# Expert rows dealt among queries, choices and gates of a bidirectional encoder block, with 16 pairs of rows held in DRAM

## The chip, the core and the metric

One core of a Trainium2 chip runs the whole layer. The metric is the device time of one execution in microseconds (us), the median of three runs. The engines are named as the profile names them: PE is the matrix engine (PEld its weight loads), DVE is VectorE, ACT is ScalarE, POOL is GpSimd and SP is the engine that issues most transfers. Each engine works through its own list of instructions in order and waits where an operand or a buffer is not ready.

## The reference

512 tokens of width 1024 in float32 pass through a mixer and then through a retrieval layer over 16384 single-neuron experts (128 rows of 128 experts).

```python
h = x
h = h + hybrid_mixer(rmsnorm(h, norm_mix_g), ...)     # HGRN2 + Hyena branches
h = h + peer_ffn(rmsnorm(h, norm_ffn_g), w_q, subkeys, u_tab, v_tab)
return rmsnorm(h, norm_final_g)

def peer_ffn(xn, ...):                                # per token, 8 heads
    s = einsum(queries, subkeys)                      # two lists of 128 scores
    s1, i1 = top_k(s[:, :, 0], 16); s2, i2 = top_k(s[:, :, 1], 16)
    top_s, pos = top_k(all sums s1 + s2, 16)          # 16 experts per head
    g = softmax(top_s)
    act = gelu(xn . u[experts]) * g
    return act . v[experts]
```

## The kernel before, in words

The mixer fills the first 760 us or so; its inner part is not touched. The retrieval layer splits the tokens into four blocks of 128. One block (GTB) is done by gathering the chosen experts' rows of `u` and `v` from DRAM, one expert of every token at a time (256 gathers by POOL, each with one DVE instruction of 1024 columns). The other three (DTB, 384 tokens) are done densely: all 128 expert rows are multiplied, and the gates, which are zero for experts not chosen, pick out the right ones.

A dense **expert row** has two halves. The first (`act_row`) takes 128 experts of `u`: a transfer `uraw` on SP's queue, a split into a high part `uh` (ACT) and a low part `ul` (DVE in the early part, POOL once the last loop runs, `looping`), 24 matmuls of 384 columns into `ps_a` (or `ps_mm` while the queries run), and a gelu on ACT into a tile `gact`. The second half (`combine`) multiplies the gated activations `gh`, `gl` with the split second factors `vh`, `vl` of the same 128 experts: 18 matmuls of 512 columns into `acc`. Activations are kept in a ring of 14 tiles of two rows each; the first KEPT pairs of rows instead go to DRAM (`C.kept`) and are read back as `gkept`.

The stages of the retrieval layer, in order:

1. **Queries** (`queries`): 16 projections of 24 matmuls, for each one the scores (L1099), and three times the sixteen best of 128 (`top16`, five DVE instructions). `STEPS` steps of the **choices** (`select`: sums of pairs, the sixteen best, softmax, the experts' numbers) run beside the later queries.
2. **Choices and gates**: for each of the three dense blocks `gates_out` builds the gates' table in 32 batches (DVE: `one`, `own`; ACT: `rows`, `Gs`; PE: 8 matmul records per batch into `ps_g`) and writes it to DRAM as `Gd`. The choices of the next block are mixed in, one step per MIX batches (`mixed`). `weave` adds up the costs that its main work yields and runs one `act_row` each time the sum passes `per`.
3. **The last loop** (`rows`): for each of 128 rows an `act_row` as long as some are left, `split_v`, for each pair `gated` (the gates `gt` read from `Gd`), and `combine`. The choices and gathers of block GTB (`gathered`) are woven in.
4. The final norm and the stores.

Program order is what a scheduling layer makes of this; where a row counts below, it is the built program's order that is shown.

Of the kernel before, what the change touches and what calls it, by code (L numbers as in the profile page):

```python
# [158 lines left out]
def block_kernel(tc, a):  # L159

    nc = tc.nc
    with ExitStack() as ctx:
# [5 lines left out]
        nc.scalar.dma_start(vec, a["vec"])  # L168
# [138 lines left out]
def hyena(C, ctx, xh, xl, raws, fill):  # L307
# [112 lines left out]
    for half in range(D // HC):  # L420
# [33 lines left out]
        for row in (0, FH):  # L454
            nc.scalar.dma_start(fw3[row : row + FH], a["f_w3"].rearrange("f (d c) -> f d c", d=2)[:, :, half * HC : half * HC + HC])
# [346 lines left out]
PER = 2.4  # L802
# [7 lines left out]
def peer(C, ctx, mh, ml):  # L810
# [74 lines left out]
    with tc.tile_pool(name="slw", bufs=2) as sw, tc.tile_pool(name="gb", bufs=1) as gb, \  # L885
            tc.tile_pool(name="go", bufs=3) as go, tc.tile_pool(name="ps_g", bufs=5, space=PSUM) as ps_g:
        def main():
            rest = [[chosen(sw, tb, part) for part in range(2) if part or k >= EARLY] for k, tb in enumerate(DTB)]
            yield from chain(*rest[0])
            for k, tb in enumerate(DTB):  # L890
                nxt = chain(*rest[k + 1]) if k + 1 < len(DTB) else iter(())
# [477 lines left out]
```

## Time and profile before

| what | value |
| --- | --- |
| time, median of 3 runs | 2113.73 us (2110.78 to 2115.68) |
| profiled execution, its own time | 2113.9 us |
| its span, first to last instruction | 2112.1 us |
| PE busy | 2058.7 us |
| DVE busy | 1736.1 us |
| ACT busy | 978.6 us |
| POOL busy | 638.2 us |
| mean granted PE clock, share of full speed | 0.992 |

A matmul counts as busy from its start to its modelled end, and successive ones overlap, so a high busy share does not by itself say that PE delivers all it can. The distance between two starts is the better measure. The clock column is the share of full speed that was granted to PE.

### The profile page before, as it was taken

The page shows a single profiled execution, that of the slowest core. Times are in us where ns is not written, and L with a number is a line of the kernel's source. Part 1 is how long each engine was busy: PE and PEld are TensorE (multiplying, and loading weights), DVE is VectorE, ACT ScalarE, POOL GpSimd, SP SyncE. Part 2 cuts the span into 40 slices and gives each one's busy share as a digit, 9 for nine tenths or more (in the row PEclk, how much of TensorE's full clock was granted, in tenths as well). Part 3 has the DMA queues.
Part 4 walks back from the last instruction along what each step waited for, and adds up shares of the span by engine and source line. Part 5 has one row for each costly group of instructions (what it writes and reads, how often), then busy time and mean ns, then how long its engine had stood idle before and what let it go on. Part 6 is the DMA issues. An engine that isn't in the chain of part 4 may idle for free. (4 is left out here: it accounts for less than half of the span.)

```text
span 2112.1 us, 29790 instructions
## 1 busy us (share of the span) xinstructions
PE 2058.7 (97%) x11109; PEld 1822.7 (86%) x11109; DVE 1736.1 (82%) x3073; ACT 978.6 (46%) x1396; POOL 638.2 (30%) x361
## 2 busy tenths in 40 slices
PE   7999999999999999979999999999999999999998
PEld 6888888888888898879988989989989998998997
DVE  6888764998998546999999988878878879778785
ACT  6555434667665623337766423333333333333333
POOL 0000000000000000000000378877777676666760
PEclk9999999999999999999999999999999999999999
DMA  6212222222212444124547689988888988888884
GB/s 199 80 51 66 70 70 94 67 65 66 70 54 81 120 151 139 61 70 168 202 180 250 192 311 344 327 318 304 321 318 301 317 311 299 316 317 324 296 286 148
DMA packets 153949, 407.68 MB, mean 193 GB/s; under 512 B 12457, under 2 KB 65451, under 8 KB 152140
## 3 DMA queue, kind: packets, MB, share of 16 engines
q1 hardware_dynamic: 110028, 255.98, 35.8%
q0 software_dynamic: 36864, 134.23, 17.6%
q10 hardware_dynamic: 6912, 15.56, 2.1%
q8 instruction: 87, 1.43, 0.3%
q14 instruction: 58, 0.48, 0.1%
HBM read 373.22 MB, written 32.51 MB: 192 GB/s over the span
## 5 line engine op out<-in xcount | busy, mean ns | idle before, releaser
L86 POOL TENSOR_TENSOR ul<-uraw,uh 128x1024 fp32r<-128x1024 f32 x100 | 265.3, 2654 | 589.7 <-DMA uraw<-in_uT 387.6
L95 PE MATMUL ps_a<-pxl,uh 128*128 128x384 f32 x1008 | 343.1, 340 | 0.0
L94 PE MATMUL ps_a<-pxh,uh 128*128 128x384 f32 x1008 | 341.8, 339 | 1.3 <-ACT gact L867 1.2
L980 PE MATMUL acc<-vl,gh 128*128 128x512 f32 x768 | 301.5, 393 | 2.1 <-DVE vl L86 2.1
L979 PE MATMUL acc<-vh,gh 128*128 128x512 f32 x768 | 299.7, 390 | 2.6 <-ACT vh L85 2.6
L981 PE MATMUL acc<-vh,gl 128*128 128x512 f32 x768 | 301.5, 393 | 0.0
L94 PE MATMUL ps_mm<-xh,whi 128*128 128x512 f32 (+1 forms) x656 | 259.1, 396 | 1.5 <-ACT xh L195 1.2
L940 DVE SCALAR_TENSOR_TENSOR xg<-grow,gw,xg 128x1024 f32<-128x1024 f32 x127 | 208.6, 1643 | 63.1 <-DMA grow<-in_v,gidx 62.0
L931 DVE SCALAR_TENSOR_TENSOR grow<-grow,xg 128x1024 f32<-128x1024 f32 x128 | 195.9, 1541 | 73.6 <-DMA grow<-in_u,gidx 73.3
L95 PE MATMUL ps_mm<-xl,whi 128*128 128x512 f32 (+1 forms) x656 | 255.0, 390 | 0.3 <-DVE xl L196 0.3
L85 ACT CAST vh<-vraw 128x1024 fp32r<-128x1024 f32 x128 | 134.3, 1050 | 252.7 <-PE acc L981 179.7
L826 POOL IOTA iota<- 128x512 bf16 x1 | 1.2, 1237 | 754.4 <-DVE gt L281 754.4
L906 POOL DMA_INDIRECT grow<-in_u,gidx x128 | 201.0, 1570 | 41.4 <-issue 19.4
L97 PE MATMUL ps_a<-pxh,ul 128*128 128x384 f32 x1008 | 200.1, 338 | 6.3 <-DVE ul L86 4.1
L85 ACT CAST uh<-uraw 128x1024 fp32r<-128x1024 f32 x128 | 134.7, 1053 | 143.5 <-PE ps_a L95 76.5
L94 PEld LDWEIGHTS ps_a<-pxh,uh 128*128 128x128 f32 x1008 | 191.1, 190 | 6.4 <-ACT gact L867 2.2
L95 PEld LDWEIGHTS ps_a<-pxl,uh 128*128 128x128 f32 x1008 | 190.9, 189 | 3.8
L86 DVE TENSOR_TENSOR vl<-vraw,vh 128x1024 fp32r<-128x1024 f32 x128 | 186.4, 1457 | 8.3 <-ACT vh L85 8.3
L97 PEld LDWEIGHTS ps_a<-pxh,ul 128*128 128x128 f32 x1008 | 176.8, 189 | 8.2 <-DVE ul L86 5.5
L906 POOL DMA_INDIRECT grow<-in_v,gidx x128 | 170.5, 1332 | 32.7 <-issue 18.3
L85 ACT CAST whi<-wraw 128x1024 fp32r<-128x1024 f32 x112 | 117.3, 1050 | 131.0 <-PE ps_mm L95 123.5
L980 PEld LDWEIGHTS acc<-vl,gh 128*128 128x128 f32 x768 | 144.6, 188 | 31.1 <-DVE vl L86 2.9
(414 smaller groups left out, 4188.8 us busy)
## 6 DMA issues: line engine op xcount, KB each, us to landing
uraw<-in_uT SPq DMA_DIRECT2D x128, 512.0 KB, 7.0
vraw<-in_v SPq DMA_DIRECT2D x128, 512.0 KB, 6.3
wraw<-in_w_in SPq DMA_DIRECT2D x80, 512.0 KB, 3.6
Gd<-Gs SPq DMA_DIRECT2D x12, 2048.0 KB, 7.2
gt<-Gd SPq DMA_DIRECT2D x32, 768.0 KB, 8.7
wraw<-in_w_q SPq DMA_DIRECT2D x16, 512.0 KB, 4.0
wraw<-in_w_b SPq DMA_DIRECT2D x8, 512.0 KB, 3.6
wraw<-in_w_a SPq DMA_DIRECT2D x8, 512.0 KB, 4.3
```

What stands on the lines that cost most here:

```text
L85: nc.scalar.copy(hi, src)
L86: return (eng or nc.vector).tensor_sub(lo, src, hi).ins
L94: nc.tensor.matmul(out, ah, bh, start=(i == 0), stop=False)
L95: nc.tensor.matmul(out, *((al, bh) if late else (ah, bl)), start=False, stop=False)
L97: nc.tensor.matmul(out, *((ah, bl) if late else (al, bh)), start=False, stop=(stop and i == n - 1))
L826: nc.gpsimd.iota(iota, pattern=[[1, P], [0, 4]], base=0, channel_multiplier=0, allow_small_or_imprecise_dtypes=True)
L906: nc.gpsimd.indirect_dma_start(out=t, out_offset=None, in_=tab, in_offset=bass.IndirectOffsetOnAxis(ap=gidx[:, j : j + 1], axis=0))
L931: nc.vector.scalar_tensor_tensor(t, t, 1.0, xg, op0=ALU.mult, op1=ALU.mult, accum_out=gdot[:, j : j + 1])
L940: nc.vector.scalar_tensor_tensor(gacc, t, gw[:, j : j + 1], gacc, op0=ALU.mult, op1=ALU.add)
L979: nc.tensor.matmul(acc[k][:, c], gh[:, ts_], vh[:, ds_], start=(r == 0), stop=False)
L980: nc.tensor.matmul(acc[k][:, c], gh[:, ts_], vl[:, ds_], start=False, stop=False)
L981: nc.tensor.matmul(acc[k][:, c], gl[:, ts_], vh[:, ds_], start=False, stop=(r == NK - 1))
```

## The change

The change has four parts.

- **Dealing.** `mixed` now passes on the costs of the choices' steps, which it swallowed before. The choices' costs are scaled by 0.39 (CHOICE) and a batch of gates costs 0.15 (BATCH); `weave` deals one expert row per 1.0. In the queries, one expert row is dealt beside each query from the eighth on, and the first halves of the choices of all three dense blocks run there, two steps per query.
- **Kept pairs.** KEPT goes from 8 to 16, so 16 pairs of rows go to DRAM and back, and LEFT from 3 to 4: 42 expert rows (2 x 16 + 14 - 4) are dealt ahead of the last loop where 27 were.
- **Placing.** The pool of the gates (`gb`) is opened ahead of the choices' pool, and `gt`, `gkept`, `gh`, `gl` move to a pool `pg` of their own that lies where `gb` lay; `pv` (`vl`, `vh`, `vraw`) lies behind it. The order of the first steps in `rows` changes.
- **The start.** The norm's weights come as one row of 1024 values and are spread over the partitions by two matmuls into PSUM, instead of a 512 KB transfer. The scaling of `x` runs in halves of 512 columns. Four small transfers for the filters are issued later.

```diff
@@ mixed
         yield c
         if i % n == n - 1:
-            next(fill, None)
+            yield next(fill, 0.0)
@@ block_kernel, mixer
-        nc.scalar.dma_start(vec, a["vec"])
...
-        gm = n1.tile([P, D], F32, name="gm")
+        gm = n1.tile([1, D], F32, name="gm")
+        gps = [C.ps_x.tile([P, 512], F32, name="ps_x") for _ in range(2)]
...
-                nc.sync.dma_start(gm, a["g_mix"].to_broadcast([P, D]))
+                nc.scalar.dma_start(gm, a["g_mix"])
+                for c, pg in enumerate(gps):
+                    nc.tensor.matmul(pg, C.ones[0:1], gm[:, c * 512 : c * 512 + 512], start=True, stop=True)
...
-            nc.vector.scalar_tensor_tensor(xn, xn, rs, gm, op0=ALU.mult, op1=ALU.mult)
+            for c, pg in enumerate(gps):
+                xc = xn[:, c * 512 : c * 512 + 512]
+                nc.vector.scalar_tensor_tensor(xc, xc, rs, pg, op0=ALU.mult, op1=ALU.mult)
@@ constants
-KEPT = 8
-LEFT = 3
+KEPT = 16
+LEFT = 4
-EARLY = 2
-STEPS = 1
+STEPS = 2
-PER = 2.4
+CHOICE = 0.39
+BATCH = 0.15
@@ peer
-    with tc.tile_pool(name="slw", bufs=2) as sw, tc.tile_pool(name="gb", bufs=1) as gb, \
+    with tc.tile_pool(name="gb", bufs=1) as gb, tc.tile_pool(name="slw", bufs=2) as sw, \
...
-            rest = [[chosen(sw, tb, part) for part in range(2) if part or k >= EARLY] for k, tb in enumerate(DTB)]
-            yield from chain(*rest[0])
+            rest = [(CHOICE * c for c in chosen(sw, tb, 1)) for tb in DTB]
+            yield from rest[0]
...
-        weave(main(), fill, PER)
+        weave(main(), fill, 1.0)
...
-    pv = rowctx.enter_context(tc.tile_pool(name="pv", bufs=2))
+    pg = rowctx.enter_context(tc.tile_pool(name="pg", bufs=2))
+    pv = rowctx.enter_context(tc.tile_pool(name="pv", bufs=AHEAD + 1))
@@ rows
+        for r in range(AHEAD - 1):
+            split_v(r)
+        for _ in range(LEFT - 1):
+            act_row()
+        gated(0)
         act_row()
-        gated(0)
-        for r in range(AHEAD):
-            split_v(r)
-            if r:
-                act_row()
+        split_v(AHEAD - 1)
         gated(1)
@@ queries
-        early = chain(*(chosen(sw, tb, 0) for tb in DTB[:EARLY]))
+        early = chain(*(chosen(sw, tb, 0) for tb in DTB))
...
-            if hp > 7:
+            if hp >= HEADS - 1:
                 run(islice(early, STEPS))
+                next(fill)
@@ gates_out
-        yield 0.4
+        yield BATCH
```

What this does to the lists is seen best where one engine's rows are few. On SP's queue, from the first query weights (`wraw<-in_w_q`) to the first stored gates (`Gd<-Gs`), the program before issues:

```order
L121 DMA wraw<-in_w_q 128x1024 x5
L846 DMA uraw<-in_uT 128x1024 x4
L121 DMA wraw<-in_w_q 128x1024
L846 DMA uraw<-in_uT 128x1024
L121 DMA wraw<-in_w_q 128x1024 x10
L846 DMA uraw<-in_uT 128x1024 x6
L1245 DMA Gd<-Gs 128x4096
```

and the changed program:

```order
L121 DMA wraw<-in_w_q 128x1024 x5
L853 DMA uraw<-in_uT 128x1024 x4
L121 DMA wraw<-in_w_q 128x1024
L853 DMA uraw<-in_uT 128x1024
L121 DMA wraw<-in_w_q 128x1024 x7
L853 DMA uraw<-in_uT 128x1024 x2
L121 DMA wraw<-in_w_q 128x1024
L853 DMA uraw<-in_uT 128x1024
L121 DMA wraw<-in_w_q 128x1024 x2
L853 DMA uraw<-in_uT 128x1024 x15
L1256 DMA Gd<-Gs 128x4096
```

Each `uraw` is one expert row's first factors. 23 of them now stand ahead of the first stored gates, where 11 stood.

On DVE, in the gates, the program before goes from one step of a choice to the next with gates between and an expert row's low part (`ul`) at the end; the rows that follow here are the first of the run, in which a softmax (`mx`, `ex`, `sm`) is mixed with gates (`one`, `own`):

```order
L1167 TENSOR_REDUCE mx<-ctop 128x4
L1175 CAST cpf<-cpos 128x64
L1228 TENSOR_TENSOR one<-iota,tr 128x1024
L1168 TENSOR_TENSOR ex<-ctop,mx 128x64
L1231 TENSOR_TENSOR own<-one,tg 128x512
L1228 TENSOR_TENSOR one<-iota,tr 128x1024 x2
L1231 TENSOR_TENSOR own<-one,tg 128x512
L1170 TENSOR_REDUCE sm<-ex 128x4
L1231 TENSOR_TENSOR own<-one,tg 128x512
L1171 RECIPROCAL sm<-sm 128x4
L86 TENSOR_TENSOR ul<-uraw,uh 128x1024
```

In the changed program the end of the last choice and the gates beside it stand so:

```order
L86 TENSOR_TENSOR ul<-uraw,uh 128x1024
L1183 TENSOR_TENSOR gate<-ex,sm 128x64
L1201 TENSOR_TENSOR exp<-one,ci 128x800
L1192 TENSOR_REDUCE eid<-exp 128x2x8 x3
L1218 CAST ii<-eid 128x128
L1219 TENSOR_SCALAR ii<-ii 128x128
L1239 TENSOR_TENSOR one<-iota,tr 128x1024 x2
L1242 TENSOR_TENSOR own<-one,tg 128x512 x2
L1239 TENSOR_TENSOR one<-iota,tr 128x1024 x2
L1242 TENSOR_TENSOR own<-one,tg 128x512
L86 TENSOR_TENSOR ul<-uraw,uh 128x1024
```

An expert row's low part now closes every handful of choice steps and batches.

On SP's queue at the end of the gates, the program before issues the first second factors (`vraw`) behind the last stored gates, two rows' `uraw` and the first `gt`:

```order
L1245 DMA Gd<-Gs 128x4096
L846 DMA uraw<-in_uT 128x1024 x2
L958 DMA gt<-Gd 128x12x128
L947 DMA vraw<-in_v 128x1024 x3
L846 DMA uraw<-in_uT 128x1024
```

and the changed program:

```order
L1256 DMA Gd<-Gs 128x4096
L853 DMA uraw<-in_uT 128x1024
L958 DMA vraw<-in_v 128x1024 x2
L853 DMA uraw<-in_uT 128x1024
L967 DMA gt<-Gd 128x12x128
```

Two `vraw` now go ahead of `gt`. On PE, five expert rows stand between the last product of the gates and the first `acc` matmul before, and nine in the changed program.

## Rows read from the trace of the kernel before

**Rows 1.** The page, part 1: busy time, share of the span, instructions.

```profile
PE 2058.7 (97%) x11109; PEld 1822.7 (86%) x11109; DVE 1736.1 (82%) x3073; ACT 978.6 (46%) x1396; POOL 638.2 (30%) x361
```

**Rows 2.** Busy time by stretch, us from the span's start.

```profile
core 0: us, PE busy (x) PEld busy (x) DVE busy (x) ACT busy (x) POOL busy (x), PEclk, DMA share, GB/s
818.40:924.70 106.30, 102.60 (x515) 86.08 (x513) 100.74 (x558) 36.67 (x67) 0.00 (x0) 0.98 0.19 60
924.70:1135.10 210.40, 195.63 (x1329) 186.29 (x1330) 208.79 (x541) 152.48 (x255) 0.00 (x0) 0.97 0.50 183
...
1247.00:1330.00 83.00, 83.00 (x415) 74.86 (x416) 74.83 (x84) 28.41 (x36) 70.10 (x38) 1.00 0.96 349
1330.00:2062.00 732.00, 732.00 (x3657) 660.73 (x3656) 599.48 (x507) 260.16 (x305) 518.32 (x297) 1.00 0.87 311
```

**Rows 3.** Timeline of PE: start, length, engine, line, operation, count.

```profile
1132.44 1.95 PE L1238 MATMUL ps_g<-rows,own 128*128 128x128 f32 x16
...
1135.10 0.33 PE L94 MATMUL ps_a<-pxh,uh 128*128 128x384 f32 x1
...
1139.26 0.33 PE L94 MATMUL ps_a<-pxh,uh 128*128 128x384 f32 x1
...
2080.18 0.39 PE L980 MATMUL acc<-vl,gh 128*128 128x512 f32 x1
...
2085.62 0.39 PE L980 MATMUL acc<-vl,gh 128*128 128x512 f32 x1
```

**Rows 4.** PE's groups of one shape, 818.4 to 1135.1 us.

```profile
L1238 PE MATMUL ps_g<-rows,own 128*128 128x128 f32 x768 | 99.7, 283 | 5.9 <-DVE own L1231 3.5 <-ACT rows L1230 1.7 <-ACT Gs L1243 0.4
...
L1099 PE MATMUL ps_x<-sk,qT 128*128 128x128 f32 x128 | 18.9, 295 | 3.1 <-ACT qT L1096 3.0
```

**Rows 5.** DVE's groups in the same stretch.

```profile
L86 DVE TENSOR_TENSOR ul<-uraw,uh 128x1024 fp32r<-128x1024 f32 x25 | 30.3, 1211 | 0.2 <-ACT uh L85 0.2
...
L1253 DVE MAX8 v<-s 128x8 f32<-128x128 f32 x63 | 16.3, 283 | 5.4 <-ACT s L1102 5.4
```

**Rows 6.** One stretch after a wait of PE; columns as in rows 2.

```profile
1067.30:1074.00 6.70, 6.34 (x27) 6.17 (x28) 6.70 (x16) 4.20 (x7) 0.00 (x0) 0.50 0.25 62
```

**Rows 7.** Timeline from the gates' end to the first gathers; in brackets the idle time before.

```profile
1156.00 0.26 ACT L1169 ACTIVATE ex<-ex 128x64 f32<-128x64 f32 x1 [6.43 <-DVE ex L1168]
...
1158.70 0.50 PE L979 MATMUL acc<-vh,gh 128*128 128x512 f32 x1 [2.63 <-ACT vh L85]
...
1221.59 1.54 POOL L906 DMA_INDIRECT grow<-in_u,gidx  x1 [9.68 <-PE ps_a L97]
...
1230.53 2.53 PE L97 MATMUL ps_a<-pxh,ul 128*128 128x384 f32 x8 [2.18 <-POOL ul L86]
```

**Rows 8.** DVE's longest waits, 1235 to 2062 us: total, times, longest.

```profile
DVE grow L931 <- DMA grow<-in_u,gidx: 65.6, 46, 5.6
DVE xg L940 <- DMA grow<-in_v,gidx: 62.0, 46, 5.7
...
DVE gkept L966 <- DMA gkept<-kept: 5.0, 2, 2.5
```

**Rows 9.** Gathered rows: ns min/median/max, first and last start; then the page's means.

```profile
L931 DVE SCALAR_TENSOR_TENSOR grow<-grow,xg x128: 1208/1215/3514, 1229.9 to 1636.8; 128x1024 f32<-128x1024 f32 x128
L940 DVE SCALAR_TENSOR_TENSOR xg<-grow,gw,xg x127: 1270/1285/3453, 1645.8 to 2061.6; 128x1024 f32<-128x1024 f32 x127
...
L86 POOL TENSOR_TENSOR ul<-uraw,uh 128x1024 fp32r<-128x1024 f32 x100 | 265.3, 2654 | 589.7 <-DMA uraw<-in_uT 387.6
...
L940 DVE SCALAR_TENSOR_TENSOR xg<-grow,gw,xg 128x1024 f32<-128x1024 f32 x127 | 208.6, 1643 | 63.1 <-DMA grow<-in_v,gidx 62.0
L931 DVE SCALAR_TENSOR_TENSOR grow<-grow,xg 128x1024 f32<-128x1024 f32 x128 | 195.9, 1541 | 73.6 <-DMA grow<-in_u,gidx 73.3
```

**Rows 10.** Timeline of the start: the first scaling and the first projection.

```profile
7.02 1.28 DVE L228 SCALAR_TENSOR_TENSOR xn<-xn,nrs,gm 128x1024 f32<-128x1024 f32 x1 [6.00 <-ACT nrs L116]
...
14.93 0.58 PE L94 MATMUL ps_mm<-xh,whi 128*128 128x256 f32 x1 [1.16 <-ACT xh L195]
```

More of the change, by code (lines that the diff above doesn't have):

```diff
@@ L172, in block_kernel @@
         C = Ctx()
+        C.fetch_vec = lambda: nc.scalar.dma_start(vec, a["vec"])
         C.nc, C.tc, C.a, C.ident, C.ones, C.vec, C.eps = nc, tc, a, ident, ones, vec, epsc
@@ L215, in mixer @@
         log_table(C)
-        gm = n1.tile([P, D], F32, name="gm")
+        C.fetch_vec()
+        gm = n1.tile([1, D], F32, name="gm")
+        gps = [C.ps_x.tile([P, 512], F32, name="ps_x") for _ in range(2)]
         xns, raws = [], []
@@ L453, in hyena @@
         fw3 = w2.tile([2 * FH, 2, HC], F32, name="fw3", bufs=1)
-        for row in (0, FH):
-            nc.scalar.dma_start(fw3[row : row + FH], a["f_w3"].rearrange("f (d c) -> f d c", d=2)[:, :, half * HC : half * HC + HC])
+        with tc.issue_after(C.turned):
+            for row in (0, FH):
+                nc.scalar.dma_start(fw3[row : row + FH], a["f_w3"].rearrange("f (d c) -> f d c", d=2)[:, :, half * HC : half * HC + HC])
         fw3h = w2.tile([2 * FH, 2, HC], F32R, name="fw3h", bufs=1)
@@ L461, in hyena @@
         decb = w2.tile([P, 2, HC], F32, name="decb", bufs=1)
-        for dr in range(2):
-            o = dr * D + half * HC
-            nc.scalar.dma_start(decb[:, dr], a["f_decay"][:, o : o + HC].to_broadcast([P, HC]))
         with tc.issue_after(C.turned):
+            for dr in range(2):
+                o = dr * D + half * HC
+                nc.scalar.dma_start(decb[:, dr], a["f_decay"][:, o : o + HC].to_broadcast([P, HC]))
             nc.scalar.activation(decb, decb, AF.Abs)
@@ L884, in peer @@
     C.ps_row, C.ps_row_name = ctx.enter_context(tc.tile_pool(name="ps_a", bufs=2, space=PSUM)), "ps_a"
[L885 removed]
+    with tc.tile_pool(name="gb", bufs=1) as gb, tc.tile_pool(name="slw", bufs=2) as sw, \
             tc.tile_pool(name="go", bufs=3) as go, tc.tile_pool(name="ps_g", bufs=5, space=PSUM) as ps_g:
         def main():
[L888 to L889 removed]
+            rest = [(CHOICE * c for c in chosen(sw, tb, 1)) for tb in DTB]
+            yield from rest[0]
             for k, tb in enumerate(DTB):
[L891 removed]
+                nxt = rest[k + 1] if k + 1 < len(DTB) else iter(())
                 yield from mixed(gates_out(C, gb, go, ps_g, k, tb, gate, eid, iota), nxt, MIX)
[L894 to L896 removed]
+        weave(main(), fill, 1.0)
+    pg = rowctx.enter_context(tc.tile_pool(name="pg", bufs=2))
+    pv = rowctx.enter_context(tc.tile_pool(name="pv", bufs=AHEAD + 1))
     swctx = ExitStack()
@@ L945, in split_v @@
     def split_v(r):
+        vl = pv.tile([P, D], F32R, name="vl")
+        vh = pv.tile([P, D], F32R, name="vh")
         raw = pv.tile([P, D], F32, name="vraw", bufs=3)
         nc.sync.dma_start(raw, a["v"][r * P : r * P + P])
-        vh = pv.tile([P, D], F32R, name="vh", bufs=AHEAD + 1)
-        vl = pv.tile([P, D], F32R, name="vl", bufs=AHEAD + 1)
         split(nc, vh, vl, raw)
@@ L956, in gated @@
         if r % GR == 0:
-            gt = pv.tile([P, NG, GR * GQ], F32, name="gt")
+            gt = pg.tile([P, NG, GR * GQ], F32, name="gt")
             nc.sync.dma_start(gt, C.Gd[:, :, r * GQ : (r + GR) * GQ].rearrange("g p x -> p g x"))
@@ L960, in gated @@
         if p in kept:
-            g = pv.tile([P, 2, ND], F32, name="gkept", bufs=1)
+            g = pg.tile([P, 2, ND], F32, name="gkept", bufs=1)
             nc.sync.dma_start(g, C.kept[kept.index(p)])
@@ L966, in gated @@
         nc.vector.tensor_mul(g4, g4, prep["gt"][:, r % GR : r % GR + 2])
-        gh = pv.tile([P, 2, ND], F32R, name="gh", bufs=3)
-        gl = pv.tile([P, 2, ND], F32R, name="gl", bufs=3)
+        gh = pg.tile([P, 2, ND], F32R, name="gh", bufs=3)
+        gl = pg.tile([P, 2, ND], F32R, name="gl", bufs=3)
         split(nc, gh, gl, g)
```

## The prediction

> **What bounds the kernel now.** I read the page's busy shares first, then the stretches, then the spacing of PE's matmuls, then the waits. PE is busy for 97% of the span [rows 1], but that is no proof of a full engine, so I priced its work by the distance between two starts. An expert row's first half takes 1139.26 - 1135.10 = 4.16 us for its 24 matmuls; 24 matmuls of 512 columns take 5.44 us, 0.227 each; 16 gate products end 1.95 us after they begin, about 0.112 apart once the last one's own length (0.283) is taken off [rows 3, 4]. PE's work can't be made less by this change: the same 128 rows, queries and gates are multiplied. Only time in which PE is held up can be won.
>
> From the queries' first scores at 818.4 us to the end of the gates at 1135.1 us the program before takes 316.7 us. PE's work in it: 768 gate records x 0.112 = 86, 128 score records x 0.112 = 14, 14 projections of 24 x 0.227 = 76, 24.8 expert rows x 4.16 = 103 (counted in the built order), transposes 1: together 281 us. So PE loses about 36 us there. DVE is busy for 100.7 + 208.8 = 309.5 us [rows 2], and of what is left 5.4 us is the wait for the first scores [rows 5]. This stage is DVE's. Choices run beside the gates without a row dealt for them, so DVE has work there that PE has nothing to set against.
>
> Two more losses follow. PE waits 2.63 us for the first second factors at 1158.7, because ACT stood 6.43 us before a softmax of the gathered block's choice (`ex`), waiting for DVE, with the cast of `vh` queued behind it; and 2.18 us at 1230.5 for a low part on POOL, which had put five gathers ahead of it from 1221.6 on [rows 7]. Counted as PE's work against the clock, the delay grows from 36 us at 1135 to 48 us at 1247: 12 us, the slower clock after each wait included. Behind a long wait PE runs at half clock, 1.2 GHz in place of 2.4, for some microseconds: a granted share of 0.50 over 6.7 us after the waits around 1065 [rows 6]. From 1247 to 2062 PE is busy without a gap at full clock [rows 2]; the last loop has nothing to win.
>
> **The change, part by part.**
>
> *Dealing.* In the changed order 38 expert rows stand ahead of the last gate product, against 25. PE's work to that point becomes 281 + 13.2 x 4.16 = 336 us. DVE splits each of the 13 (1.21 us, [rows 5]): 309.5 + 13 x 1.21 = 325 us. So over the whole stage PE becomes the bound, by 11 us. That is an average; what decides is where DVE is furthest behind. I added up both engines' work instruction by instruction in each built order, with the spacings of the trace. In the order before, DVE's sum is ahead of PE's by at most 30.7 us, near the gates' end; with the 5.4 us at the start this makes 36, which is what the trace shows, so I trust the same sum for the changed order. There it is 9 us at the first gate products, 11.8 us at worst early in the second block, and negative from the third block on. PE's loss is then 11.8 + 5.4 = 17 us. The same work (38 rows, all gates) cost 316.7 + 13.2 x 4.16 = 371.6 before and costs 336 + 17 = 353 after: **18 us won**. Bounds: 36 won if the small lags vanish in PE's queue; 5 if the choices moved into the queries hold up the scores, or two falls of the clock in which PE is the bound (3.4 us each at most, half of [rows 6]) come on top.
>
> *Placing, and more rows ahead of the last loop.* Nine expert rows instead of five, 37 us of PE's work instead of 21, lie between the last gate product and the first `acc`. The gathered block's choice comes 20 us or more ahead of PE's need in the same sum, and ACT's list has the casts of the first two `vh` ahead of `ex`. The five gathers on POOL still stand in a row, but DVE, which sets the time of their indices, is some 30 us ahead of PE there instead of 15 us behind. Against this, the two first `vraw` are issued only when the last gate products have left their memory, and ACT's cast waits for them in line: a loss of 0 to 5 us, with the clock's share. I take 2 of the 12 us as left: **10 us won**, bounds 4 and 12.
>
> *Kept pairs.* Eight more pairs of 384 KB go to DRAM and back. Of the writes ACT only issues the transfers, hidden in an engine with 152 of 210 us busy [rows 2]. Reading back cost DVE 5.0 us of waits before [rows 8], beside work of PE; twice that stays hidden as long as the last loop is PE's, and if that cover is gone costs 5 us more.
>
> *The last loop.* It has 17 expert rows less (81 against 98 behind the first `acc`), but still all 256 gathers, one every 3.25 us from 1229.9 to 2061.6 [rows 9]. Between those two points PE's work shrinks by about 62 us (15 rows), from 832 to 770. DVE was busy 74.8 + 599.5 = 674 of 815 us from 1247 to 2062 [rows 2] and waited 128 us for gathered rows [rows 8]. The mean of its instructions on gathered rows is 1541 and 1643 ns where the median is 1215 and 1285, with single ones at 3.5 us [rows 9]: they are held up by something. 15 of the 100 low parts leave POOL; if these are what holds DVE, (326 x 128 + 358 x 127) ns / 100 = 0.87 us per low part, 13 us go. DVE then needs 661 in 753 us, 88%, with 92 us left for waits that took 128. It ran at 74.8 of 83 us, 90%, from 1247 to 1330, at 349 GB/s, and PE did not wait once [rows 2]. I take **0**; the bound is the case in which the gathers keep their pace, 62 us lost less the 20 us or so by which DVE may run behind at the end.
>
> The Trainium skill (SBUF — State Buffer, section "SBUF: two separate sides") says that DVE instructions with two SBUF inputs and POOL's share one pair of ports under an exclusive lock, and that the loser blocks for the whole instruction. The 3.5 us in [rows 9] agree with it: 1.2 us of work plus most of a low part's 2.65 us on POOL. By that rule each low part taken from POOL frees at most 2.65 us of DVE, 40 us for 15, and the last loop would have more room than I gave it; the sum would stay as it is.
>
> *The start.* The 512 KB of norm weights leave SP's queue, which brings the first weights of the mixer forward by one transfer; but DVE's list now begins with their low part, ahead of the first scaling, which started at 7.02 us [rows 10]. Eight scalings of 512 columns out of PSUM replace four of 1.28 us; at half the length each they cost the same. The first projection (14.93 us, [rows 10]) needs the same casts on ACT as before. I take 0, bounds 3 us won and 3 lost.
>
> The sum, against the profiled execution's own 2113.9 us (median 2113.7, so nothing to correct): 2113.9 - 18 - 10 + 0 + 0 = **2086 us**. With the bounds of the stages but PE still bound in the loop: 2113.9 - 36 - 12 - 3 = 2063 to 2113.9 - 5 - 4 + 3 + 5 = 2113.
>
> **The rivals.**
>
> *The loop becomes DVE's (slower).* For it: DVE's 83% and 128 us of waits fill 802 of 815 us, and the waits may depend on the gathers' latency, which grows with the DMA engines' load (0.87 to 0.96 in [rows 2]). If the 832 us of gathering don't shrink at all, 62 - 20 = 42 us are lost: 2128. It decides once more than 28 us of the 62 stay. Against it: the 90% from 1247 to 1330. A part of it, 5 to 20 us lost, is more likely than the whole: about 2098.
>
> *The dealing is too coarse.* Choices of the first halves in the queries put three blocks' softmaxes and gelus on ACT in turn, and DVE's lag in the second block could grow by a clock fall each time. Then 5 to 8 us are won there and 4 behind it: 2103.
>
> *Everything fits.* DVE's lags vanish between the rows, and the start gains: 36 + 12 + 1: 2065.
>
> *The change does nothing* because another engine held the stage: ACT is busy 152 of 210 us and its sums stay 70 us or more ahead of PE; I give it nothing.
>
> **The numbers.** Forecast as worked out, 2076 to 2096: 0.55. Everything fits, 2063 to 2076: 0.10. Too coarse, 2096 to 2109: 0.12. Loop partly DVE's, 2090 to 2109: 0.14. Loop fully DVE's, above 2114: 0.07; within 0.2% of before, between these: 0.02. About 0.2% (4 us) is what a measurement of this kernel tells from no change. Faster by more: 0.55 + 0.10 + 0.12 + 0.14 = 0.91, less 0.04 for what no row here shows: 0.87. Same 0.05, slower 0.08. The range runs from 2068 to 2106; half of "everything fits" and about 0.12 above it are left out.
>
> **What would show it.** Right: DVE busy shares near full until the second block of gates and falling in the third, PE without gaps from there; the first `acc` without a wait and without a stretch at half clock near it; gathers every 3.0 us in the loop, DVE's waits for them near 90 us, PE without gaps. Wrong: PE waits for `vl`, `gl` or POOL's `ul` in the loop; `own` waits in the third block; ACT waiting for `vraw` for more than 5 us at the gates' end.

## Result and profile after

The changed kernel takes 2098.5 us (median of 4 runs, 2097.2 to 2101.3) against 2113.6 us (4 runs, 2110.8 to 2115.7) on the same chip: ratio 0.9931, 95% interval 0.9914 to 0.9948. 15 us are won where 28 were forecast. The profiled execution took 2099.15 us, its span 2097.0.

The page of the changed kernel, part 1, and its stretches, with columns as in [rows 1, 2]:

```profile
PE 2051.3 (98%) x11113; PEld 1822.1 (87%) x11113; DVE 1718.4 (82%) x3092; ACT 984.2 (47%) x1400; POOL 597.5 (28%) x346
```

```profile
818.00:924.00 106.00, 105.27 (x552) 91.19 (x551) 100.45 (x514) 46.60 (x72) 0.00 (x0) 1.00 0.32 100
924.00:1000.00 76.00, 67.37 (x355) 63.87 (x354) 71.12 (x314) 29.90 (x45) 0.00 (x0) 0.91 0.27 85
1000.00:1090.00 90.00, 87.81 (x623) 87.45 (x622) 89.64 (x186) 68.04 (x118) 0.00 (x0) 1.00 0.63 220
1090.00:1180.00 90.00, 90.00 (x671) 89.56 (x670) 69.79 (x121) 70.67 (x123) 0.00 (x0) 1.00 0.60 226
1180.00:1240.00 60.00, 53.31 (x279) 51.18 (x277) 58.97 (x199) 25.69 (x32) 20.47 (x7) 0.94 0.70 228
1247.00:1330.00 83.00, 83.00 (x411) 74.21 (x410) 70.17 (x76) 27.89 (x33) 58.08 (x33) 1.00 0.89 316
1330.00:2062.00 732.00, 732.00 (x3612) 654.83 (x3611) 612.28 (x556) 260.94 (x305) 515.14 (x301) 1.00 0.91 328
...
929.52:936.35 6.83, 4.43 (x17) 4.43 (x17) 6.83 (x19) 2.32 (x5) 0.00 (x0) 0.50 0.27 78
1216.24:1223.07 6.83, 6.01 (x19) 6.01 (x20) 6.71 (x21) 2.54 (x5) 2.75 (x1) 0.50 0.52 166
```

The third block of gates (1090 to 1180 us) and the last loop are PE's without a gap. Three places lose time: 924 to 1000, 1180 to 1240, and a spot at 807 just ahead of the first stretch. At each of them PE runs at half clock for a stretch, granted share 0.50 for 6.83 us; there are four such stretches, and the last two lines show two of them. Timelines of the changed kernel (start, length, engine, line, operation; in brackets the idle time before and what ended it) show the waits:

```profile
800.38 0.34 ACTq L1102 DMA_DIRECT2D sk<-in_skT  x1
800.84 1.06 ACTq L1085 DMA_DIRECT2D hd<-h  x1
809.25 1.28 DVE L1088 SCALAR_TENSOR_TENSOR h<-h,prs,gfn 128x1024 f32<-128x1024 f32 x1 [4.29 <-DMA hd<-h]
...
921.15 1.28 ACT L1180 ACT_TABLE_LOAD   x1 [0.39 <-ACT gact L874]
930.19 0.26 ACT L1180 ACTIVATE ex<-ex 128x64 f32<-128x64 f32 x1 [7.76 <-DVE ex L1179]
930.35 1.03 ACT L85 CAST whi<-wraw 128x1024 fp32r<-128x1024 f32 x1
931.29 0.58 ACT L1106 COPY qT<-ps_mm 128x512 f32<-128x512 f32 x1
931.92 2.07 PE L1109 MATMUL ps_x<-sk,qT 128*128 128x128 f32 x8 [5.51 <-ACT qT L1106]
...
934.52 0.60 DVE L1199 TENSOR_TENSOR one<-pio,cpf 128x800 bf16<-128x800 bf16 x1
...
968.26 1.28 ACT L1180 ACT_TABLE_LOAD   x1
969.55 0.26 ACT L1180 ACTIVATE ex<-ex 128x64 f32<-128x64 f32 x1
969.83 1.28 ACT L874 ACT_TABLE_LOAD   x1
971.12 0.49 ACT L874 ACTIVATE gact<-ps_mm 128x384 f32<-128x384 f32 x1
971.67 0.69 PE L94 MATMUL ps_a<-pxh,uh 128*128 128x384 f32 x1 [3.12 <-ACT gact L874]
...
1201.06 2.86 POOL L86 TENSOR_TENSOR ul<-uraw,uh 128x1024 fp32r<-128x1024 f32 x1 [3.38 <-ACT uh L85]
1201.70 2.65 DVE L1199 TENSOR_TENSOR one<-pio,cpf 128x800 bf16<-128x800 bf16 x1
1209.24 2.52 DVE L86 TENSOR_TENSOR vl<-vraw,vh 128x1024 fp32r<-128x1024 f32 x1
1215.79 0.83 ACT L85 CAST gh<-gact 128x768 fp32r<-128x768 f32 x1 [8.10 <-DVE gact L975]
1216.53 0.48 ACT L874 ACTIVATE gact<-ps_a 128x384 f32<-128x384 f32 x1
1217.06 0.69 PE L94 MATMUL ps_a<-pxh,uh 128*128 128x384 f32 x1 [5.60 <-ACT gact L874]
```

At 807 DVE's scaling of `h`, in place, waits until the 512 KB of `h` have been written; that write was issued 0.46 us behind 1 MB of subkeys and held the scaling to 8.4 us after its issue. At 922 ACT stands 7.76 us before an exponential that DVE has not fed, with the weight's cast and the query's copy queued behind it, and PE waits for that copy. At 968 the next exponential costs PE a wait of 3.12 us, and not by waiting for DVE: a table load of 1.28 us stands on either side of it, ahead of the gelu that PE needs. At 1207 ACT stands 8.10 us before a cast of `gh`, with the gelu queued behind it whose PSUM buffer PE wants.

To compare kernels, PE's loss in a stretch is worked out as in the prediction: the distance between two starts less the usual one (0.227 us for 512 columns, 0.173 for 384, 0.112 for 128), summed. What PE loses at half clock is in it. A gap, here and below, is the distance between the two starts on either side of a wait. In before and e10 the gates end at about 1135 us, not 1180, so their last two columns hold other work.

| us | 790–818 | 818–1090 | 1090–1180 | 1180–1240 | time, us | ratio to before (95%) |
|---|---|---|---|---|---|---|
| before | 4.1 | 34.0 | 8.3 | 4.4 | 2113.6 | |
| after | 6.9 | 20.1 | 0.2 | 10.1 | 2098.5 | 0.9931 (0.9914–0.9948) |
| e1 exp later | 4.4 | 14.8 | 0.2 | 9.0 | 2091.2 | 0.9893 (0.9878–0.9909) |
| e2 gh later | 5.6 | 19.4 | 0.2 | 2.8 | 2092.4 | 0.9902 (0.9886–0.9917) |
| e3 choice early | 4.9 | 19.8 | 7.0 | 5.1 | 2103.0 | 0.9947 (0.9934–0.9961) |
| e4 sk behind | 1.0 | 20.0 | 0.3 | 10.1 | 2093.5 | 0.9903 (0.9888–0.9918) |
| e5 not placed | 5.6 | 19.8 | 0.2 | 10.4 | 2097.5 | 0.9924 (0.9911–0.9937) |
| e6 27 rows | 6.7 | 20.1 | 36.2 | 11.6 | 2137.6 | 1.0108 (1.0087–1.0129) |
| e7 e1+e2+e4 | 1.0 | 14.8 | 0.3 | 2.9 | 2081.0 | 0.9846 (0.9833–0.9859) |
| e8 first choice | 1.0 | 17.8 | 0.3 | 3.7 | 2085.9 | 0.9873 (0.9859–0.9888) |
| e9 rows earlier | 1.0 | 17.8 | 0.2 | 6.1 | 2092.2 | 0.9898 (0.9883–0.9913) |
| e10 before, sk | 1.0 | 34.1 | 8.6 | 4.2 | 2110.0 | 0.9985 (0.9976–0.9994) |
| e11 DVE low parts | 5.6 | 19.5 | 0.3 | 0.1 | 2095.0 | 0.9913 (0.9898–0.9928) |
| e12 rows, order | 1.0 | 14.4 | -0.1 | 3.6 | 2081.9 | 0.9849 (0.9836–0.9863) |

The intervals are some 3 us to either side (e10, with more runs, 2), so the times of two changed kernels that lie under 4 us apart are not told apart; the traces are. The kernel before, measured again beside each group of runs, took 2113.4 to 2113.8 us, so times of different groups can be compared.

### The profile page after: what moved, and what is told of

It reads as the page before. It is cut to its first block, busy times and chain, and to the rows that moved or that the text cites. A ratio compares the mean times of both kernels' runs of the same rounds, so it can differ in the third digit from the quotient of the medians.

```text
span 2097.0 us, 29798 instructions
## 1 busy us (share of the span) xinstructions
PE 2051.3 (98%) x11113; PEld 1822.1 (87%) x11113; DVE 1718.4 (82%) x3092; ACT 984.2 (47%) x1400; POOL 597.5 (28%) x346
## 5 line engine op out<-in xcount | busy, mean ns | idle before, releaser
L86 POOL TENSOR_TENSOR ul<-uraw,uh 128x1024 fp32r<-128x1024 f32 x85 | 222.6, 2619 | 606.2 <-PE ps_a L97 447.7
L94 PE MATMUL ps_a<-pxh,uh 128*128 128x384 f32 x936 | 318.8, 341 | 9.8 <-ACT gact L874 9.8
L95 PE MATMUL ps_a<-pxl,uh 128*128 128x384 f32 x936 | 317.8, 340 | 0.0
L949 DVE SCALAR_TENSOR_TENSOR xg<-grow,gw,xg 128x1024 f32<-128x1024 f32 x127 | 188.6, 1485 | 42.7 <-DMA grow<-in_v,gidx 41.5
L94 PEld LDWEIGHTS ps_a<-pxh,uh 128*128 128x128 f32 x936 | 178.0, 190 | 13.9 <-ACT gact L874 10.8
L915 POOL DMA_INDIRECT grow<-in_v,gidx x128 | 175.5, 1371 | 37.8 <-issue 22.1
L97 PE MATMUL ps_a<-pxh,ul 128*128 128x384 f32 x936 | 181.9, 335 | 0.0
L95 PEld LDWEIGHTS ps_a<-pxl,uh 128*128 128x128 f32 x936 | 178.0, 190 | 3.2
L86 DVE TENSOR_TENSOR wlo<-wraw,whi 128x1024 fp32r<-128x1024 f32 x112 | 136.7, 1221 | 45.7 <-ACT whi L85 23.5
L990 PEld LDWEIGHTS acc<-vh,gl 128*128 128x128 f32 x768 | 144.1, 188 | 30.1
```

Of the source, the lines that this page charges most:

```text
L86: return (eng or nc.vector).tensor_sub(lo, src, hi).ins
L94: nc.tensor.matmul(out, ah, bh, start=(i == 0), stop=False)
L95: nc.tensor.matmul(out, *((al, bh) if late else (ah, bl)), start=False, stop=False)
L97: nc.tensor.matmul(out, *((ah, bl) if late else (al, bh)), start=False, stop=(stop and i == n - 1))
L915: nc.gpsimd.indirect_dma_start(out=t, out_offset=None, in_=tab, in_offset=bass.IndirectOffsetOnAxis(ap=gidx[:, j : j + 1], axis=0))
L949: nc.vector.scalar_tensor_tensor(gacc, t, gw[:, j : j + 1], gacc, op0=ALU.mult, op1=ALU.add)
```

## The experiments

Theory A: ACT takes its list in order, so an instruction that waits for DVE holds up the casts, copies and gelus behind it, and with them PE. Rival B: DVE is late by itself, as the prediction's sum has it (17 us), and a wait taken from ACT comes back as one for DVE. The others are for the stalls at 1211 and 807. Theory C: DVE is late there because POOL's low parts hold DVE's instructions with two inputs. Theory D: DVE's list at the loop's beginning is too long. Theory E: the write of `h` is late because it goes behind the subkeys.

**e1: the exponential behind the next query's copies.**

```diff
@@ select: after the subtraction of the maximum
-    nc.scalar.activation(ex, ex, AF.Exp)
+    yield 0.0
+    with C.tc.issue_after(C.copied):
+        nc.scalar.activation(ex, ex, AF.Exp)
@@ queries: scores() notes its last copy on ACT
-            nc.scalar.copy(s0[:, hp], pt[:, GTB])
+            C.copied = nc.scalar.copy(s0[:, hp], pt[:, GTB]).ins
...
```

The cut (`...`) lets a choice's steps beside a query stop at the `0.0`.

> The softmax's exponential of a choice dealt into the queries is put on ACT behind the next query's copies. Theory A (ACT's order): at 922.4 us ACT stood 7.76 us in front of an exponential whose input DVE had not made, with a weight cast and the query's copy queued behind it; with the exponential behind them PE's gaps at 926.1 (5.84 us) and 968.2 (3.46 us) fall under 1.5 us each, the two half-clock stretches go (about 3.4 us each), PE's loss from 818 to 1090 us falls from 20 to 8-12 us, and the time is 2085 to 2091 us against 2098.5. Theory B (DVE's lag, the prediction's own sum of 17 us): DVE is late by itself; the loss reappears as waits for low parts (wlo, ul) or for own, stays 17 to 20 us in the stage, and the time is 2095 to 2100 us.

The gap of 5.84 us at 926 is gone. That of 3.46 us at 968 is not: in e1 it stands at 957 and is 6.55 us long. It is at the same exponential, that of the choice ahead of the gates, which has no query's copies to go behind. In after this one cost PE its two table loads; in e1 ACT reaches it some 11 us earlier, and now it waits 3.09 us for DVE as well. The stretch and the timeline in e1:

```profile
924.00:1000.00 76.00, 68.66 (x396) 65.46 (x395) 75.97 (x303) 36.98 (x57) 0.00 (x0) 0.96 0.33 103
```

```profile
961.74 0.26 ACT L1188 ACTIVATE ex<-ex 128x64 f32<-128x64 f32 x1 [3.09 <-DVE ex L1185]
962.01 1.28 ACT L874 ACT_TABLE_LOAD   x1
963.31 0.49 ACT L874 ACTIVATE gact<-ps_mm 128x384 f32<-128x384 f32 x1
963.85 0.69 PE L94 MATMUL ps_a<-pxh,uh 128*128 128x384 f32 x1 [6.21 <-ACT gact L874]
```

5.3 us of the stage's 20.1 go, so ACT's order cost that much, net. The 14.8 us that stay lie between what A (8 to 12) and B (17 to 20) had. The time falls by 7.3 us, more than the stage explains: in the profiled runs 2.5 us of the difference stand at 807, which this edit leaves alone. DVE is now busy for all of 924 to 1000 (75.97 of 76 us, 71.12 before the edit): ACT's hold had come back on DVE, which in after stood 4.88 us ahead of 957.28 for ACT's copy `s`. The rest of the loss does not answer to this edit.

**e2: the third cast of `gh` behind the gelu.** The edit traces `gated(2)` at r = 1 instead of r = 0; on ACT one `gh` and one gelu change places, and PE's list stays as it is.

```diff
-            if r % 2 == 0 and r // 2 + 2 < NP:
+            if r == 1:
+                gated(2)
+            if r and r % 2 == 0 and r // 2 + 2 < NP:
                 gated(r // 2 + 2)
```

> The third pair of second factors (gated(2)) is traced one row later, which on ACT swaps one cast of gh with the gelu behind it and leaves PE's order as it is. Theory A (ACT's order): at 1207.7 us ACT stood 8.10 us in front of that cast with the gelu behind it, and this made PE's gap of 5.94 us at 1211; the gap falls under 2 us, the half clock behind it goes, 5 to 9 us are won, time 2090 to 2094 us. Theory C (DVE behind POOL's low parts): DVE is late with everything there, PE's next need from DVE (gl, vl at the first acc, or the next cast of gh) stops it instead; under 2 us won, time 2096.5 to 2100 us.

The timeline of ACT in e2, and the stretch:

```profile
1205.16 0.49 ACT L874 ACTIVATE gact<-ps_a 128x384 f32<-128x384 f32 x1
1216.15 0.84 ACT L85 CAST gh<-gact 128x768 fp32r<-128x768 f32 x1 [10.50 <-DVE gact L975]
```

```profile
1180.00:1240.00 60.00, 57.84 (x309) 54.24 (x308) 59.14 (x203) 28.02 (x35) 21.55 (x8) 1.00 0.72 235
```

ACT waits longer for DVE than before the edit (10.50 against 8.10 us) and PE hardly at all (a gap of 1.46 us against 5.94), because the gelu is out by then. The clock stays full. Theory A holds here: what counted was not the wait but what was queued behind it.

**e3: half of the gathered block's choice beside the third block of gates.**

```diff
-                nxt = rest[k + 1] if k + 1 < len(DTB) else iter(())
+                nxt = rest[k + 1] if k + 1 < len(DTB) else own_choice(sw)
@@ own_choice: top16 of 8 halves and chosen(sw, GTB, 0), all at cost 0.0; gathered() begins with part 1
```

The last line tells in words what the edit adds.

> The first half of the gathered block's choice is taken out of the last loop's beginning and dealt at no cost beside the third block of gates, where DVE is busy 70 of 90 us (1090 to 1180). Theory D (DVE's list at the loop's beginning is too long): without that choice gh is made in time, the gap of 5.94 us at 1211 and the 1.43 us at 1201 go with the half clock, 7 to 11 us are won, time 2087 to 2092 us, and no new gap over 1.5 us stands between 1090 and 1180. Theory C (POOL's low parts hold DVE's two-input instructions): four low parts still stand at 1193 to 1211, DVE's products still take 2 to 2.7 us in place of 1, a gap of 3 us or more stays, time 2094 to 2098 us. If the 20 us of DVE's idle time in the third block are not free, waits for own appear there and up to 10 us are lost: 2099 to 2109.

A miss for D: 4.5 us slower than after, in the last of the three ranges. The third block in e3:

```profile
1090.00:1180.00 90.00, 86.00 (x625) 85.35 (x624) 84.23 (x179) 70.01 (x121) 0.00 (x0) 0.96 0.56 216
```

DVE's 20 idle us there (in after mostly waits for ACT's `uh`, one of 8.59 us and seven of under 2.3) were not free: with the choice in DVE's list ACT waits 3.40 us for `one` at 1105, and the choice's exponential with its two table loads stands on ACT from 1109.96 to 1112.81 us, ahead of a copy `Gs` that PE wants. A gap of 4.27 us appears at 1110, while 3.53 us stay at 1207. There ACT again stood before an exponential (3.54 us) with gelus behind it.

**e4: the subkeys behind the last write of `h`.**

```diff
-            nc.scalar.dma_start(C.hd[ts_], h)
+            C.stored = nc.scalar.dma_start(C.hd[ts_], h).ins
@@
-        nc.scalar.dma_start(sk, a["skT"])
+        with tc.issue_after(C.stored):
+            nc.scalar.dma_start(sk, a["skT"])
```

> The 1 MB transfer of the subkeys (sk) is issued behind the last write of h instead of just ahead of it. Theory E (the write is late behind sk, and the scaling in place waits for it): after, the last scaling of h started at 809.25 us, 8.4 us after its write was issued at 800.84; now the write takes 4.4 us as those of other blocks, the scaling starts near 805, PE's gap of 4.00 us at 806.7 falls under 1.5 us and the half clock (6.83 us at half, 3.4 lost) goes or shrinks: 4 to 7 us won, time 2091.5 to 2094.5. Rival: the write is as slow with the weights of the experts beside it; gap 2 us or more, or the first scores at 818 now wait for sk: within 2 us of 2098.5.

The timeline of e4 at that place:

```profile
802.24 0.33 ACTq L1085 DMA_DIRECT2D hd<-h  x1
803.86 0.34 ACTq L1103 DMA_DIRECT2D sk<-in_skT  x1
805.44 1.29 DVE L1088 SCALAR_TENSOR_TENSOR h<-h,prs,gfn 128x1024 f32<-128x1024 f32 x1 [0.42 <-DMA hd<-h]
```

The scaling starts 3.2 us after the write's issue instead of 8.4, PE has no gap and no half clock there: 5.0 us, as theory E said.

**e5: the placing undone.** Pools, order of `split_v` and of the loop's first rows as before; dealing, 16 pairs and the start as after.

```diff
-    with tc.tile_pool(name="gb", bufs=1) as gb, tc.tile_pool(name="slw", bufs=2) as sw, \
+    with tc.tile_pool(name="slw", bufs=2) as sw, tc.tile_pool(name="gb", bufs=1) as gb, \
@@
-    pg = rowctx.enter_context(tc.tile_pool(name="pg", bufs=2))
-    pv = rowctx.enter_context(tc.tile_pool(name="pv", bufs=AHEAD + 1))
+    pv = pg = rowctx.enter_context(tc.tile_pool(name="pv", bufs=2))
...
@@ rows()
-        for r in range(AHEAD - 1):
+        act_row()
+        gated(0)
+        for r in range(AHEAD):
             split_v(r)
-        for _ in range(LEFT - 1):
-            act_row()
-        gated(0)
+            if r:
+                act_row()
         act_row()
-        split_v(AHEAD - 1)
         gated(1)
```

> After with the placing undone: choices' pool ahead of the gates' again, the pool of second factors and gated pairs in one as before, and the old order of the first rows of the last loop; dealing, 16 kept pairs and the start stay. The prediction's term says that the placing won 10 us: 2108 to 2109 us. What the trace of after says (10.1 us of PE's loss between 1180 and 1240 us against 12.6 in the like stretch of before): about 2 us, 2098 to 2103 us, with a first acc that waits again and POOL's five gathers in a row or not. A time under 2097 would say that the new placing made the stall at 1211 itself.

Nothing is lost: 2097.5 against 2098.5 us. Between 1180 and 1240 PE loses 10.4 us in place of 10.1, in two gaps of 3.64 and 3.60 us for ACT's gelus. The waits of before (`acc` for `vh`, a row for POOL's low part behind the gathers) don't come back. The placing is worth nothing that this measurement tells.

**e6: 27 rows to deal.** `KEPT = 8`, `LEFT = 3`, all else as after.

> After with 8 kept pairs and LEFT 3, so that 27 rows in place of 42 can be dealt ahead of the last loop, at the same costs. If the number of rows is what the dealing won by (PE's loss falls from 35 to 20 us to the gates' end), the rows run out in the second block of gates, own waits stand from there to the end of the third as in before, 8 to 15 us are lost: 2106 to 2114 us. If the gain came from the place of the choices alone (first halves in the queries), and the kept transfers cost what they saved: 2096 to 2101 us.

39 us slower than after, where 8 to 15 were expected. The 27 rows are used up at 1072 us, ahead of the third block, and PE then has mostly gate products:

```profile
1090.00:1180.00 90.00, 59.86 (x435) 57.24 (x435) 54.56 (x89) 53.70 (x99) 29.21 (x4) 0.83 0.46 182
```

But the long waits there are of another kind, which the expectation did not have. Lines of four engines:

```profile
1066.05 30.56 SPq L853 DMA_DIRECT2D uraw<-in_uT  x4
1077.60 18.65 POOL L86 TENSOR_TENSOR ul<-uraw,uh 128x1024 fp32r<-128x1024 f32 x1 [322.25 <-ACT uh L85]
1096.66 23.87 SPq L1256 DMA_DIRECT2D Gd<-Gs  x4
1105.34 1.56 ACT L1254 COPY Gs<-ps_g 128x512 f32<-128x512 f32 x3 [14.81 <-DMA Gd<-Gs]
1105.98 6.58 PE L1249 MATMUL ps_g<-rows,own 128*128 128x128 f32 x40 [14.26 <-ACT Gs L1254]
```

With the early rows gone, rows of the last loop move up beside the gates, and their low parts are on POOL. One of them, 2.45 us in the median of this run, lasts 18.65 us here: DVE is busy with the gates' products, which have two inputs, for all of 1077.60 to 1094.06 us, and the low part ends 2.19 us after they stop. SP's transfers of `uraw` take until 0.4 us behind its end, the stored gates `Gd` are queued behind them, ACT waits for a `Gs` tile that is still to be stored, and PE waits for ACT. The same comes again at 1144: a low part of 17.68 us that ends 2.19 us after DVE's products, and a wait of PE of 13.50 us.

The stage to 1090 loses 20.1 us in both kernels. So the new costs can't do with 27 rows in this program; what the 15 rows are worth without this stall, and what the old costs would do with 42 rows, no run shows.

**e7: the three edits together.**

> After with the three edits of e1, e2 and e4 together. If the three losses stand in a row on PE (nothing else is late behind them): 2098.5 - 7.3 - 6.1 - 5.0 = 2080 us, 2083 at most, since part of e1's 7.3 was a shorter gap at 806. If DVE's lag takes their place in the queries (theory B), the sum falls short: 2084 to 2088 us.

2081.0 us, the sum of the three within a microsecond: three losses in a row on PE, none hiding another. By the table the three edits take 5.3, 7.3 and 5.9 us out of their own stages, 18.5 together, and e7 takes 18.3 out of all. This kernel beats both: 17.5 us under after, 32.7 under before.

**e8: the exponential of the first choice beside the gates behind one more gelu.** As e7, with

```diff
-            yield from rest[0]
+            yield from (c or 0.25 for c in rest[0])
@@ act_row: a gelu counts as a copy that an exponential may go behind
-        last_gelu[0] = nc.scalar.activation(
+        C.copied = last_gelu[0] = nc.scalar.activation(
```

> As e7, and in the first block's second-half choice, which in e1 held ACT at 957.4 us (a table load, 3.09 us for DVE, the exponential, a table load, then the gelu that PE had waited 6.21 us for), the exponential is put behind one more expert row's gelu. Theory A (ACT's order): this gap of 6.55 us and its half clock (6.8 us) go too, 6 to 10 us below e7: 2070 to 2076 us. Theory B (DVE's lag of 11.8 us early in the second block): own waits of the same size appear at the first gate products, at most 3 us below e7: 2077 to 2083 us.

PE's longest waits in e8, 940 to 1240 us: total, times, longest.

```profile
PE ps_g L1239 <- DVE i L1233: 4.6, 1, 4.6
PE ps_g L1260 <- ACT rows L1252: 4.0, 2, 3.9
```

The gap at 955 falls from 6.52 to 0.92 us, and two new ones stand at 967 (4.92 us) and 1049 (4.21 us): for DVE's expert numbers, and for ACT's `rows` after ACT had itself waited 5.88 us for DVE. The time is 4.9 us longer than e7's, outside the range of either theory; of the two B is nearer. But the edit does more than was meant, since a gelu counts for every later choice too: the second block's exponential runs at 1069.04 us, 27.5 us after DVE has fed it, where in e7 it was 1.1 us. So e8 doesn't test the first choice alone.

**e9: two rows earlier.** As e7, with the costs of that choice multiplied:

```diff
-            yield from rest[0]
+            yield from (c * 1.54 for c in rest[0])
```

> As e7, and the costs of the first block's second-half choice are multiplied by 1.54 in all, so that two expert rows more stand ahead of the first gate products and two fewer behind them. Each row is 4.16 us of PE's work and 1.21 us of DVE's: DVE's lag behind PE's need falls by 2 x 2.95 = 5.9 us there. Theory B (what is left of the loss in the queries and gates after e7, 14.8 us, is DVE's lag): the gap at 955 (6.52 us) shrinks to under 3, the own waits at 985 to 1045 go, 5 to 8 us below e7's 2081.0: 2073 to 2076. Theory A (ACT's order alone makes the gap at 955): the gap stays as long, 0 to 2 us are won. If the two rows are missed later, as 15 rows were in e6, own waits appear in the third block: 2082 to 2088.

A miss, outside all three ranges: the gap at 954 stays (6.54 us). The edit could hardly touch it: counted by their matmuls, 11 rows stand ahead of that exponential in e7 and in e9, and the two rows come between it and the first gate product (18 rows in place of 16). So B is not tested there. Later the two rows are missing: gaps of 4.79 us at 1040 (for DVE's `own`) and 4.45 at 1197 (for ACT's gelu), and 4.8 us more than after are lost between 1240 and 1400.

**e10: the edit of e4 in the kernel before.**

> The kernel before with the 1 MB transfer of the subkeys issued behind the last write of h, as in e4. If the stall at 807 us stands in both kernels (before: a gap of 1.87 us and 3.41 us at half clock), 2 to 5 us are won here too: 2108.5 to 2111.5 against 2113.6. If it is the change that made it, nothing is won: 2112.5 to 2114.5.

3.7 us are won (1.3 to 5.1 by the interval), the gap of 1.87 us and its half clock are gone. The stall stands in both kernels; in the changed one and e1 to e3, e5, e6 and e11, which leave that place alone, its gap is 2.7 to 4.0 us.

**e11: low parts on DVE until the loop's first `acc`.** `looping.append(True)` moves behind `gated(1)`, so the rows ahead of it keep `ul` on DVE.

> After with the low parts of the expert rows traced ahead of the last loop's first acc left on DVE (1.2 us each) in place of POOL (2.4 to 2.9 us each). Theory C (DVE is late at 1207 us because POOL's four low parts from 1193.57 to 1210.7 hold its two-input instructions, one of them 2.65 us in place of 0.57, another 2.5 in place of 1.2): DVE is through earlier, ACT's wait for gact falls from 8.1 us to under 5, 2 to 6 us are won: 2092.5 to 2096.5. If four more low parts on DVE cost what POOL took, within 2 us of 2098.5.

```profile
1180.00:1240.00 60.00, 60.00 (x325) 57.07 (x324) 59.38 (x191) 27.64 (x34) 10.35 (x4) 1.00 0.74 240
```

This stretch of e11 has no loss (0.1 us) and full clock; ACT's longest wait for `gact` falls from 8.1 to 4.1 us, though DVE has more in its list. 5.46 us come back at 1274, for a `vl` on DVE, so only 3.5 us are won, less than two times are told apart by. The stretch itself speaks for C.

**e12: e8 and e9 together, with 17 pairs.** `(c * 1.54 or 0.30 for c in rest[0])`, `KEPT = 17`.

> As e9, with the exponential of the first block's second-half choice behind one more gelu as in e8, and with 17 kept pairs, so that the two rows dealt earlier are two rows more and are not missed later. Alone, e8 (order) moved the loss of the stage from a wait for ACT to waits for DVE, and e9 (rows) left the wait for ACT as it was. If the two stand in a row (ACT's order first, DVE's lag of 5 us behind it), both go now: PE's loss from 924 to 1000 us falls from 8.5 us to under 4, that of 818 to 1090 from 17.8 to 6-11 us, and the time is 2073 to 2079 us, below e7's 2081.0. If DVE's lag simply moves on to the next block whatever is dealt, the gap at 1040 to 1050 (4.2 to 4.8 us) stays or grows and the time is 2081 to 2088 us.

```profile
924.00:1000.00 76.00, 69.10 (x369) 64.64 (x368) 75.86 (x286) 31.01 (x46) 0.00 (x0) 0.96 0.39 116
1000.00:1090.00 90.00, 90.00 (x646) 89.97 (x645) 84.31 (x182) 72.15 (x121) 0.00 (x0) 1.00 0.60 219
```

A miss again for the first range, 2081.9 us: from 1000 to 1180 nothing is lost any more, but 11.9 us are, from 924 to 1000, where DVE is busy for 75.86 of 76 us. The longest gap, 5.38 us, is the wait for the first gate products, for which ACT waits 7.80 us for DVE's `one`. As in e8 the order of every later choice is changed too. In all five runs without the wait at 926 (e1, e7, e8, e9, e12) the stage to 1090 still loses 14.4 to 17.8 us.

## Why the prediction was half right

- **The last loop stays PE's: right.** PE is without gaps from 1247 to 2062 us. Gathered rows are taken every 3.07 us (1266.3 to 2047.9 us for 255 steps; 3.0 was forecast), and DVE waits 88.5 us for them (forecast 90; [rows 8] had 128). The wait for kept pairs was mis-sized (10 us), and stayed hidden as said; it measured 36.1 us in 10 waits. What holds DVE's instructions on gathered rows over their medians fell from 87 to 65 us, with 85 low parts on POOL in place of 100; the prediction had 13 of these 22. DVE's longest waits in the loop of after:

```profile
DVE grow L940 <- DMA grow<-in_u,gidx: 47.0, 34, 4.3
DVE xg L949 <- DMA grow<-in_v,gidx: 41.5, 35, 3.4
DVE gkept L975 <- DMA gkept<-kept: 30.7, 9, 6.3
DVE gkept L975 <- issue: 5.4, 1, 5.4
```

- **Dealing, 18 us: the mechanism right as far as it went, the size 14.6.** Before loses 35 us from 818 to 1135; after 20.3 to 1180, where 17 were forecast, so 14.6 are won. By the sum, the loss that stays was to be DVE's lag alone. The runs divide it otherwise: 5.3 us are ACT's order (e1), which the prediction excluded with "its sums stay 70 us or more ahead of PE". A sum over a stage says that ACT has time to spare; it doesn't say that ACT may stand for 8 us with a copy behind it that PE needs now. The 14.4 to 17.8 us that no reordering removed fit the lag of 17, and DVE is busy for 97% of 818 to 1000 in e7 (100.89 and 75.97 of 182 us). That speaks for the bound that was named, but no run took work from DVE there, so it is argued and not shown. How much more rows there could save stays open; e9 and e12 moved rows, and the loss moved with them. What of the 14.6 us came from the 15 more rows and what from the choices' new place is not shown either, since e6 has a stall of its own.
- **Placing, 10 us: the step that failed.** Around the first `acc` 12.6 us were lost before (1135 to 1250) and 10.1 are lost after (1180 to 1240), and the placing has no part in the difference (e5). The first `acc` indeed comes without a wait, as forecast, but it does so in e5 too; and a new wait begins 13 us ahead of it, with half clock until 1223.07 us, 1 us ahead of the first `acc`. The step that "the gathered block's choice comes 20 us or more ahead of PE's need in the same sum" adds up DVE and PE, and has no term for POOL's low parts beside DVE's products, nor for ACT's list ahead of the gelu. Four low parts on POOL stand beside them from 1193.6 to 1210.7 us: `one` of 800 elements takes 2.65 us beside one of them and 0.60 in the queries. So `gact` was late, and ACT's order passed it on to PE. e2 (a gelu first) and e11 (no POOL beside it) each remove the loss in the stretch. The rule of the Trainium skill named in the prediction (SBUF — State Buffer, section "SBUF: two separate sides") speaks of this pair of engines, and the trace agrees: the `one` of 2.65 us began 0.64 us behind the start of POOL's low part of 2.86 us and ended 0.43 us behind its end. The prediction used it for the last loop, where it changed nothing, and not here.
- **The start, 0 us: right by itself, 0.7 us won** (the gap at 282.7 us comes at 281.9, that at 807.4 at 806.7). Around 807 the profiled run then lost 2.8 us more than the one before (6.9 against 4.1; a gap of 4.00 us in place of 1.87, 6.83 us at half clock in place of 3.41); the code there is the same, and e10 shows the stall in both kernels. Why it is longer in the changed one is open (the seven runs that leave it alone have 2.7 to 4.0 us); that it hangs on the order of two transfers is shown (e4, e10).
- **The sum again, in the profiled runs:** 14.6 (dealing) + 2.5 (around the first `acc`) + 0.7 (start) - 2.8 (at 807) = 15.0, against 14.75 us between them.
- **The rivals.** That choices in the queries put softmaxes "on ACT in turn", with a clock fall each time, had 0.12; it is the nearest to what happened, with 2103 us, and should have been part of the forecast. The time lies in the stated range, 2068 to 2106, by the room that such rivals had in it, not by the sum, whose own band was 2076 to 2096. The sign was there: [rows 7] showed the same wait, 6.43 us before a softmax's `ex`.

## What to carry over

Ask of an engine with time to spare not how much, but what stands in its list behind each instruction that waits for the bound engine: here two exponentials (at 930 and 1198 us) and one cast, of 0.3 to 0.8 us, passed DVE's lateness on to PE, a third exponential cost PE its table loads, and e7 won 17.5 us by changing orders alone. A sum over a built order needs the durations of the place where it is used, with the neighbour engines at work, not the undisturbed ones. Twice a wait that was removed came back in part at another place: in e1 the next gap grew from 3.46 to 6.55 us, in e11 5.46 us stood at 1274. So the loss of whole stages is to be compared, not the gap. And a slower run has to be read in its own trace before it counts for a theory: e6 lost 39 us, and its longest waits came by a chain over POOL, SP and ACT that the kernel with 42 rows doesn't have.

## What was not expected of the hardware

An exponential of 0.26 us between gelus costs ACT two table loads of 1.28 us more: 2.8 us in all. A write of 512 KB let its reader go on 3.2 us after its issue when 1 MB was issued behind it, and 8.4 us after it when the 1 MB went 0.46 us ahead (6.3 us in the run of before). A low part on POOL that takes 2.45 us in the median took 18.65 and 17.68 us beside DVE's back-to-back products with two inputs, and ended 2.2 us after these stopped (e6). Behind the gap of 5.84 us at 926 PE ran 6.83 us at a share of 0.50 in after and 3.41 us in e2; behind a gap of 2.89 us in e8 the clock stayed full. 6.83 us at that share cost up to 3.4 us more, and the gap and this stretch together are most of what e4 and e2 took out of their stages (5.9 and 7.3 us).
